# Tying the loads of h, and their squares, to the newest products in the MLP of a hybrid decoder layer

## The chip, the cores and the metric

The kernel runs on one core of a Trainium2 chip. The metric is the device time of one execution in microseconds (us); a lower time is better. Engines are named as in the profile: PE multiplies matrices, DVE is the vector engine, ACT the scalar engine (activations and copies out of PE's accumulators), POOL the general engine, SP issues most of the transfers.

## The reference, cut to what matters

One decoder layer over 2064 tokens (16 meta tokens and 2048 others) of width 1024, in 32-bit floats. A mixing half comes first (a gated convolution group beside a state-space group, a norm per group, one output projection, added to the residual stream). What follows is the half that the change touches:

```python
h = h + mixed @ w_out[i]                     # end of the mixing half
hn = rms_norm(h, norm_ffn_g[i])              # the norm ahead of the MLP
up = causal_dwconv(hn @ w_up[i], ffn_conv_w[i], ffn_conv_b[i])   # 2 x 2816 columns, width 3
a, val = up[..., :D_FF], up[..., D_FF:]
h = h + (silu(a) * val) @ w_down[i]
y = rms_norm(h, norm_final_g)                # the last norm
return y[:, N_META:]
```

`rms_norm` divides each token by the root of the mean of its 1024 squares and multiplies by a gain per column.

## The kernel before, in words

**Data.** Everything stands with features on the 128 partitions and tokens along the free dimension. The residual stream h lies in device memory as `h_d`, 128 partitions x 8 groups of features x 2064 tokens. The mixing half ends by storing h there (L957). The MLP adds its result to `h_d` by transfers that accumulate (L1510).

**Products.** Each 32-bit operand is split into a high part and a low remainder, and a product is three matmuls (high x high, high x low, low x high). Weights are loaded raw (`wr`), split by ACT into `wh` (L248) and by DVE into `wl` (L109), and then used. `Feed` keeps up to four split tiles and up to three raw ones ready (L1226 to L1266).

**The MLP** runs over three blocks of 676 or 688 tokens, each in two halves (columns c = 0 and 1). In a block, 22 feature tiles f are made by `up(f)`: seven forms of twelve matmuls each (a Strassen-like scheme with seven products instead of eight; X, Y, z1, z2 are accumulators), copied out by ACT (L1447, L1449, L1454, L1456) or added by DVE into the tiles `g` and `v` of the tag z. X and Y are used by several forms, so PE has to wait for their evictions. Then `activate` does the convolution, silu and the gate, and splits the outcome. Chunks of 4, 4, 4, 3, 3 and 4 tiles f are multiplied by w_down one chunk late: after the first `up` of chunk ci, `down(ci - 1, ...)` makes the eight output groups m (0 and 1 together, then one by one). ACT copies each to `ev` (L1506), and POOL issues the accumulating transfer to `h_d` (L1510).

**The norms beside it.** Small generators do the rest in the gaps; `prep` holds them in a queue, and `prep.step()` lets the first go on to its next `yield`. A step is made after each `up(f)` with f below 18 and after each down, two after the pair.
- `prep_rs(b)` (L1108) makes the inverse root mean squares of block b ahead of its MLP, one half after the other, through `inv_rms_from` (L216): two loads of h (L221), four yields, two squares in place by ACT (L227), three adds by DVE (L109), a sum over partitions by PE (`st_f`, L188), a power on POOL, and a broadcast by PE (`sb_f`, L208) that ACT copies to `rsk`. Block 0's runs in the mixing half, block 1's is queued before the MLP begins, block 2's in block 1.
- `finish(b)` (L1349) is the last norm of block b, run in the next block, again half by half: two loads (L1354), four yields, two squares into other buffers `ysq` (L1358), adds, `st_y`, `sb_y`, the scaling (L1369) and two stores to `y` (L1372). Block 2 has another way (L1375).
- `prep_mlp(b)` (L1122) loads h once more (L1134), scales it (L1139) and makes the split operands of the next block.

The loads' tiles and the squares share the tag "sq", a ring of four buffers in the MLP.

**What sets the order.** The program is traced in the order in which it is written, but each engine gets a list that a planner lays out when the program is built: it goes through the instructions with modelled durations, gives each engine what is ready in its model, prefers what stands earlier in the program, and fills an idle engine with what stands later. Dependences through data and buffers are kept by semaphores. At run time each list is worked through as it was laid out. So a load or a square may stand well ahead of its place in the program if nothing that it depends on forbids it.

Of the kernel before, what the change touches and what calls it, by code (L numbers as in the profile page):

```python
# [14 lines left out]
AF = mybir.ActivationFunctionType  # L15
ALU = mybir.AluOpType

P = 128
D = 1024
# [38 lines left out]
def layer_kernel(ctx, tc, xq, pk, w_in, w_glu, w_out, w_up, w_down, ssm_s, ssm_m, y):  # L58
    nc = tc.nc
    V, S, T, G = nc.vector, nc.scalar, nc.tensor, nc.gpsimd  # L60
    dma = nc.sync.dma_start
# [13 lines left out]
    h_d = dram.tile([P, KD, L], F32, name="h_d")  # L75
# [32 lines left out]
    def tt(out, a, b, op):  # L108
        V.tensor_tensor(out, a, b, op=op)  # L109
# [37 lines left out]
    def half_tile(n, name, tag="xt", bufs=3):  # L147
        return xp_.tile([P, 4, QM], F32, tag=tag, bufs=bufs, name=name)[:, :, :n]
# [32 lines left out]
    def inv_rms_of(s, nfeat, n, name, out=None, keep=False):  # L181
        sl, starts = slices(n)
        nj = len(starts)
        ps = aux_tile(f"st_{name}")
        terms = s if isinstance(s, list) else [s]
        for j, o in enumerate(starts):
            for i, a in enumerate(terms):
                T.matmul(  # L188
                    ps[:sl, j : j + 1], a[:, o : o + sl], ones[:, 0:1], start=i == 0, stop=i == len(terms) - 1
                )  # L190
        return (yield from inv_rms_at(ps[:sl, :nj], starts, nfeat, n, name, out, keep))
# [24 lines left out]
    def inv_rms_from(srcs, n, name, out=None):  # L216

        ts = []
        for i, src in enumerate(srcs):
            ts.append(half_tile(n, f"sq_{name}_{i}", tag="sq", bufs=SQ))  # L220
            dma(out=ts[i], in_=src)  # L221
        yield
        yield
        yield
        yield
        for t in ts:
            S.activation(t, t, AF.Square)  # L227
        a, b = ts
        tt(a, a, b, ALU.add)
        tt(a[:, 0:2, :], a[:, 0:2, :], a[:, 2:4, :], ALU.add)  # L230
        tt(a[:, 0, :], a[:, 0, :], a[:, 1, :], ALU.add)
        yield
        yield
        return (yield from inv_rms_of(a[:, 0, :], D, n, name, out))
# [58 lines left out]
    prep, ssm = Side(), Side()  # L293
# [812 lines left out]
    rs_f = [{} for _ in range(3)]  # L1106

    def prep_rs(b):  # L1108

        first, ni, _ = BLOCKS[b]  # L1110
        n = ni // 2
        rsk = rs_tile(f"rsk_{b}")
        for c in range(2):
            out = rsk[:, c, :n]
            s0 = first + c * n
            rs_f[b][c] = yield from inv_rms_from([h_d[:, i * 4 : i * 4 + 4, s0 : s0 + n] for i in range(2)], n, f"f{b}{c}", out)
            yield

    hf = [{} for _ in range(3)]
# [91 lines left out]
    for i in range(3):  # L1211
        c = C_FW + i * 44 + FT
# [131 lines left out]
    def y_at(b, c):  # L1344
        tb, ni, no = BLOCKS[b]
        n = no // 2
        return tb + ni - no + c * n, n

    def finish(b):  # L1349
        for c in range(2):  # L1350
            s0, n = y_at(b, c)
            xs, sq = ([half_tile(n, f"{k}_{b}_{c}_{i}", tag="sq", bufs=4) for i in range(2)] for k in ("y", "ysq"))
            for i, a in enumerate(xs):
                dma(out=a, in_=h_d[:, i * 4 : i * 4 + 4, s0 : s0 + n])  # L1354
            for _ in range(4):
                yield
            for a, q in zip(xs, sq):
                S.activation(q, a, AF.Square)  # L1358
            yield
            q = sq[0]  # L1360
            tt(q, q, sq[1], ALU.add)
            tt(q[:, 0:2, :], q[:, 0:2, :], q[:, 2:4, :], ALU.add)
            tt(q[:, 0, :], q[:, 0, :], q[:, 1, :], ALU.add)
            yield
            rs = yield from inv_rms_of(q[:, 0, :], D, n, f"y{b}{c}")
            yield
            for i, a in enumerate(xs):
                for k in range(4):
                    V.scalar_tensor_tensor(  # L1369
                        out=a[:, k], in0=a[:, k], scalar=col(C_FIN + 4 * i + k), in1=rs, op0=ALU.mult, op1=ALU.mult  # L1370
                    )
                dma(out=y[:, i * 4 : i * 4 + 4, s0 - META : s0 - META + n], in_=a)  # L1372
                yield
# [16 lines left out]
    def ev2_tile(name):  # L1390
        return fp.tile([P, MAX_OUT], F32, tag="ev2", bufs=3, name=name)

    prep.add(prep_rs(1))
    feed.pump()
    acc = []
    for b in range(3):
        tb, ni, no = BLOCKS[b]
        n, nn = ni // 2, no // 2
        o = 2 if b else 0
# [39 lines left out]
        def up(f, end=False):  # L1439
            g, v = (z_tile(f"z_{b}_{f}_{i}")[:, :nz] for i in range(2))  # L1440
            g2, v2 = two(g[:, o:]), two(v[:, o:])
            xy = xy_tile(f"xy_{b}_{f}")
            X, Y = xy[:, 0, :n], xy[:, 1, :n]
            z1, z2 = (ps_z.tile([P, 512], F32, tag="z", name=f"pz_{b}_{f}_{i}")[:, :n] for i in range(2))
            w = feed.take()
            form(X, w, 1, "b11", stop=False)
            S.activation(g2[:, 0, :], X, AF.Copy)  # L1447
            form(z2, w, 0, "t4")
            S.activation(v2[:, 0, :], z2, AF.Copy)  # L1449
            feed.done()  # L1450
            work()
            w = feed.take()
            form(Y, w, 0, "t1", stop=False)
            S.activation(v2[:, 1, :], Y, AF.Copy)  # L1454
            form(X, w, 1, "t2", start=False, stop=False)
            S.activation(g2[:, 1, :], X, AF.Copy)  # L1456
            feed.done()
            work()
            w = feed.take()
            form(Y, w, 0, "b22", start=False)  # L1460
            tt(g2[:, 1, :], Y, g2[:, 1, :], ALU.add)
            feed.done()
            w = feed.take()
            form(z1, w, 1, "b21")
            tt(g2[:, 0, :], z1, g2[:, 0, :], ALU.add)
            work()
            later.append(activate(f, (g, v)))
            form(X, w, 0, "t3", start=False)
            if end:
                work()  # L1470
            tt(v2, X.unsqueeze(1).to_broadcast([P, 2, n]), v2, ALU.add)
            feed.done()
            if f < f0_last:
                prep.step()

# [4 lines left out]
        def down(ci, ms, cs=(0, 1), into=None):  # L1480

            f0, nk = chunk_of[ci]
            todo, whole = [], {}
            for i, m in enumerate(ms):
                name = f"dn_{b}_{ci}_{m}_{cs[0]}"
                if i < 2:
                    ps = xy_tile(name)
                    whole[m] = ps[:, :, :nn]
                    ps = [ps[:, c, :nn] for c in cs]
                else:  # L1490
                    ps = [ps_z.tile([P, 512], F32, tag="z", name=f"{name}_{c}")[:, :nn] for c in cs]
                todo.append((m, ps, feed.take()))

            def rhs_down(k, i):
                return tuple(a[:, cs[i] * nn : (cs[i] + 1) * nn] for a in act[f0 + k])

            for ks in (range(nk - 1), range(nk - 1, nk)) if len(ms) > 1 else (range(nk),):
                for m, ps, w in todo:
                    product(ps, w, rhs_down, nk, ks=ks)
            for m, ps, _ in todo:  # L1500
                feed.done()
                s0 = tb + ni - no
                if into is None:
                    ev = ev2_tile(f"ev_{b}_{ci}_{m}")[:, :no]
                    if m in whole:
                        S.activation(two(ev), whole[m], AF.Copy)  # L1506
                    else:
                        for c in cs:
                            S.activation(two(ev)[:, c], ps[c], AF.Copy)
                    G.dma_start(out=h_d[:, m, s0 : s0 + no], in_=ev, accum_op=ALU.add)  # L1510
                else:
                    for i, c in enumerate(cs):
                        tt(into(m, c), ps[i], into(m, c), ALU.add)

        first_pair = [(0, 1)] + [(m,) for m in range(2, KD)]
        for ci, (f0, nk) in enumerate(chunk_of):
            if ci == last and b < 2:
                prep.drain()
                prep.add(prep_mlp(b + 1, hf[b + 1]))
            for f in range(f0, f0 + nk):  # L1520
                up(f, f == f0 + nk - 1 and ci == last)
                if f == f0 and ci:
                    for ms in first_pair:
                        down(ci - 1, ms)
                        work()
                        prep.step(len(ms))
            if ci == last:
                settle()
# [11 lines left out]
        else:  # L1540
            s0, _ = y_at(b, 0)
            for i in range(4):
                t = f32(hl_tile(QM, f"acc_{i}", **(xh2 if i < 2 else {})))
                for m in range(2):
                    dma(
                        out=t[:, 2 * m : 2 * m + 2, :nn],
                        in_=h_d[:, 2 * i + m, s0 : s0 + no].rearrange("p (c t) -> p c t", c=2),
# [6 lines left out]
            for c in range(2):  # L1554
                s = half_tile(nn, f"tail_sum{c}", tag="sq", bufs=4)[:, 0, :]
                for ms in first_pair if c == 0 else [(m,) for m in range(KD)]:
                    down(last, ms, (c,), rows)
                    for m in ms:
                        q = s if m == 0 else z_tile(f"tq_{c}_{m}")[:, :nn]
# [90 lines left out]
```

## Time and profile before

| | |
|---|---|
| median of 3 runs | 2223.89 us (2220.8 to 2225.02) |
| the profiled execution | 2220.69 us, its span 2218.9 us |
| PE busy | 2121.5 us, 96% of the span |
| DVE, ACT busy | 1682.3 us (76%), 1102.1 us (50%) |
| mean granted clock of PE | 0.98 |
| MLP | from about 745 us to the end |

The rows of the profile give times from the start of the span. A row of waits reads: engine, output and line that waited, what ended the wait, total us, number, longest. A group of instructions reads: line, engine, operation, output <- inputs, shapes, count, then busy us and mean ns of one, then idle time of the engine before them. Tiles carry the program's names: `y`, `ysq` and `sq_f` are the tiles of the norms, `z` and `ev` those of up and down. L109 and L248 are helpers that many places call, so tiles tell more than lines there. A transfer's row on SP is its issue; it lands later.

### The profile page before, as it was taken

What the parts mean: (1) busy time and instruction counts of PE and PEld (TensorE: products, weight loads), DVE (VectorE), ACT (ScalarE), POOL (GpSimd) and SP (SyncE); (2) the same over time, 40 slices, a digit from 0 to 9 for tenths busy, and PEclk for the clock granted to TensorE, in tenths of its full rate; (3) what the DMA queues carried; (4) which work ended last, traced back from release to release, by engine and by line L of the source; (5) the groups of instructions that cost most, each with busy time, mean ns of one, the idle gap of its engine ahead of it and who ended that gap; (6) DMA issues with size and microseconds to landing.
All of it is one profiled execution on the core that took longest, in us unless ns stands there. A gap on an engine that the chain in (4) does not pass through costs nothing. (4 is left out here: it accounts for less than half of the span.)

```text
span 2218.9 us, 33122 instructions
## 1 busy us (share of the span) xinstructions
PE 2121.5 (96%) x13012; PEld 2061.5 (93%) x13012; DVE 1682.3 (76%) x2507; ACT 1102.1 (50%) x1651; POOL 151.4 (7%) x174
## 2 busy tenths in 40 slices
PE   7997999999899999999999899899999899999996
PEld 7997999998899999999999899899999899999996
DVE  8896499858956887686768869677868868667776
ACT  4135333337423555465556555455556555455555
POOL 0000000000000000100111010100111010110000
PEclk9998999999999999999999999999999999999998
DMA  7376544351576334624555262733555262653463
GB/s 241 108 219 164 145 149 150 108 178 53 162 233 202 134 105 120 142 80 112 129 130 130 91 169 76 211 107 87 139 128 141 82 170 62 158 120 95 101 170 113
DMA packets 170749, 300.28 MB, mean 135 GB/s; under 512 B 32416, under 2 KB 104800, under 8 KB 170464
## 3 DMA queue, kind: packets, MB, share of 16 engines
q1 hardware_dynamic: 149856, 246.41, 35.9%
q0 software_dynamic: 19584, 47.52, 12.6%
q10 hardware_dynamic: 1152, 4.23, 0.5%
q8 instruction: 102, 1.67, 0.3%
q14 instruction: 55, 0.45, 0.1%
HBM read 214.29 MB, written 83.82 MB: 134 GB/s over the span
## 5 line engine op out<-in xcount | busy, mean ns | idle before, releaser
L109 DVE TENSOR_TENSOR wl_up<-wr_up,wh_up 128x1024 fp32r<-128x1024 f32 x198 | 241.6, 1222 | 138.7 <-ACT wh_up L248 132.8
L138 PE MATMUL dn<-ah,wh_dn 128*128 128x344 f32 (+1 forms) x1024 | 327.8, 324 | 10.4 <-ACT ah L248 8.9
L139 PE MATMUL dn<-al,wh_dn 128*128 128x344 f32 (+1 forms) x1024 | 324.7, 320 | 0.4 <-DVE al L109 0.3
L248 ACT ACTIVATE wh_up<-wr_up 128x1024 fp32r<-128x1024 f32 x198 | 209.5, 1059 | 197.3 <-DVE wr_up L109 53.1
L1409 PE MATMUL xy<-h_t,wh_up 128*128 128x344 f32 (+1 forms) x792 | 263.9, 333 | 12.9 <-ACT z L1447 7.9
L1411 PE MATMUL xy<-h_t,wl_up 128*128 128x344 f32 (+1 forms) x792 | 254.0, 321 | 0.0
L1410 PE MATMUL xy<-l_t,wh_up 128*128 128x344 f32 (+1 forms) x792 | 253.7, 320 | 0.0
L142 PE MATMUL dn<-ah,wl_dn 128*128 128x344 f32 (+1 forms) x1024 | 247.3, 320 | 0.0
L138 PEld LDWEIGHTS dn<-ah,wh_dn 128*128 128x128 f32 x1024 | 193.6, 190 | 14.4 <-ACT ah L248 9.7
L1510 POOL DMA_DIRECT2D h_d<-ev x136 | 118.3, 870 | 1233.5 <-ACT ev L1506 1221.0
L139 PEld LDWEIGHTS dn<-al,wh_dn 128*128 128x128 f32 x1024 | 194.2, 190 | 1.8 <-DVE al L109 1.0
L1409 PE MATMUL xy<-h_b,wh_up 128*128 128x344 f32 (+1 forms) x528 | 176.5, 335 | 13.7 <-ACT z L1456 12.2
L1409 PEld LDWEIGHTS xy<-h_t,wh_up 128*128 128x128 f32 x792 | 149.8, 189 | 30.7 <-ACT z L1454 16.4
L142 PEld LDWEIGHTS dn<-ah,wl_dn 128*128 128x128 f32 x1024 | 178.1, 190 | 0.0
L1410 PE MATMUL xy<-l_b,wh_up 128*128 128x344 f32 (+1 forms) x528 | 169.9, 322 | 0.0
L1411 PE MATMUL xy<-h_b,wl_up 128*128 128x344 f32 (+1 forms) x528 | 168.6, 322 | 0.0
L248 ACT ACTIVATE wh_dn<-wr_dn 128x512 fp32r<-128x512 f32 (+1 forms) x144 | 85.5, 594 | 134.7 <-issue 52.5
L1410 PEld LDWEIGHTS xy<-l_t,wh_up 128*128 128x128 f32 x792 | 150.6, 190 | 0.0
L1411 PEld LDWEIGHTS xy<-h_t,wl_up 128*128 128x128 f32 x792 | 150.4, 190 | 0.0
L115 DVE SCALAR_TENSOR_TENSOR g<-z,pv,g 128x688 f32<-128x688 f32 (+1 forms) x132 | 122.3, 927 | 22.9 <-ACT g L1414 22.2
L109 DVE TENSOR_TENSOR wl_dn<-wr_dn,wh_dn 128x512 fp32r<-128x512 f32 (+1 forms) x144 | 92.5, 644 | 58.7 <-ACT wh_dn L248 57.4
L115 DVE SCALAR_TENSOR_TENSOR v<-z,pneg,v 128x688 f32<-128x688 f32 (+1 forms) x132 | 122.4, 928 | 9.4 <-ACT v L1414 8.1
(401 smaller groups left out, 5361.9 us busy)
## 6 DMA issues: line engine op xcount, KB each, us to landing
wr_up<-in_w_up SPq DMA_DIRECT2D x132, 512.0 KB, 5.4
h_d<-ev POOLq DMA_DIRECT2D x88, 344.0 KB, 6.8
wr_dn<-in_w_down SPq DMA_DIRECT2D x96, 256.0 KB, 2.7
wr_cw<-in_w_in SPq DMA_DIRECT2D x36, 512.0 KB, 4.5
h_d<-ev POOLq DMA_DIRECT2D x48, 336.0 KB, 6.6
x_c<-in_xq SPq DMA_DIRECT2D x16, 688.0 KB, 6.4
wr_dn<-in_w_down SPq DMA_DIRECT2D x48, 192.0 KB, 2.3
xr<-in_xq SPq DMA_DIRECT2D x24, 344.0 KB, 3.9
```

The costliest lines, as they stand in the source:

```text
L109: V.tensor_tensor(out, a, b, op=op)
L115: V.scalar_tensor_tensor(out=out, in0=a, scalar=s, in1=b, op0=ALU.mult, op1=ALU.add)
L138: T.matmul(ps[c], hi[:, k, :], xh, start=k == 0, stop=False)
L139: T.matmul(ps[c], hi[:, k, :], xl, start=False, stop=False)
L142: T.matmul(ps[c], lo[:, k, :], xh, start=False, stop=k == nk - 1)
L248: S.activation(hi, t, AF.Copy)
L1409: T.matmul(ps, hi[:, j, :], xh[:, j, :], start=start and j == 0, stop=False, **kw)
L1410: T.matmul(ps, hi[:, j, :], xl[:, j, :], start=False, stop=False, **kw)
L1411: T.matmul(ps, lo[:, j, :], xh[:, j, :], start=False, stop=j == 3, **kw)
L1510: G.dma_start(out=h_d[:, m, s0 : s0 + no], in_=ev, accum_op=ALU.add)
```

## The change

`hold(t)` copies one column of `mark[0]`, a product, into the first column of a tile that is then overwritten: the load or the square that fills the tile has to come after the copy, and the copy after the product. `mark[0]` is set anew, as the program is traced, by each `up` (a column of its tile `g`, which DVE writes at L1465 of before) and by each `down` that stores (a column of `ev`). `norm_h` is the part of `finish` from its loads to its inverse root mean squares, with a hold ahead of each load and of each square. `finish` calls it, and `prep_rs` calls it for blocks 1 and 2, which so square into buffers of their own and not in place. `prep_rs(1)` is queued after `up(0)` of block 0 and no longer ahead of the MLP; its first step then follows `up(1)`.

```diff
@@ prep_rs @@
-            rs_f[b][c] = yield from inv_rms_from([h_d[:, i * 4 : i * 4 + 4, s0 : s0 + n] for i in range(2)], n, f"f{b}{c}", out)
+            srcs = [h_d[:, i * 4 : i * 4 + 4, s0 : s0 + n] for i in range(2)]
+            if b == 0:
+                rs_f[b][c] = yield from inv_rms_from(srcs, n, f"f{b}{c}", out)
+            else:
+                _, rs_f[b][c] = yield from norm_h(srcs, n, f"f{b}{c}", out)
             yield
@@ ahead of finish @@
+    mark = [None]
+
+    def hold(t):
+
+        V.tensor_copy(t[:, 0, 0:1], mark[0])
+
+    def norm_h(srcs, n, name, out=None):
+
+        xs, sq = ([half_tile(n, f"{k}_{name}_{i}", tag="sq", bufs=4) for i in range(2)] for k in ("y", "ysq"))
+        for a, src in zip(xs, srcs):
+            hold(a)
+            dma(out=a, in_=src)
+        for _ in range(4):
+            yield
+        for a, q in zip(xs, sq):
+            hold(q)
+            S.activation(q, a, AF.Square)
+        yield
+        q = sq[0]
+        tt(q, q, sq[1], ALU.add)
+        tt(q[:, 0:2, :], q[:, 0:2, :], q[:, 2:4, :], ALU.add)
+        tt(q[:, 0, :], q[:, 0, :], q[:, 1, :], ALU.add)
+        yield
+        rs = yield from inv_rms_of(q[:, 0, :], D, n, name, out)
+        return xs, rs
@@ finish @@
-            ...
-            rs = yield from inv_rms_of(q[:, 0, :], D, n, f"y{b}{c}")
+            srcs = [h_d[:, i * 4 : i * 4 + 4, s0 : s0 + n] for i in range(2)]
+            xs, rs = yield from norm_h(srcs, n, f"y{b}{c}")
@@ ahead of the loop over blocks @@
-    prep.add(prep_rs(1))
     feed.pump()
@@ up, at its end @@
             tt(v2, X.unsqueeze(1).to_broadcast([P, 2, n]), v2, ALU.add)
             feed.done()
+            mark[0] = g[:, o : o + 1]
             if f < f0_last:
                 prep.step()
@@ down, where it stores @@
                     G.dma_start(out=h_d[:, m, s0 : s0 + no], in_=ev, accum_op=ALU.add)
+                    mark[0] = ev[:, 0:1]
@@ loop over f @@
                 up(f, f == f0 + nk - 1 and ci == last)
+                if b == f == 0:
+                    prep.add(prep_rs(1))
```

More of the change, by code (lines that the diff above doesn't have):

```diff
@@ L1351, in finish @@
             s0, n = y_at(b, c)
[L1352 to L1364, printed above, removed]
-            rs = yield from inv_rms_of(q[:, 0, :], D, n, f"y{b}{c}")
+            srcs = [h_d[:, i * 4 : i * 4 + 4, s0 : s0 + n] for i in range(2)]
+            xs, rs = yield from norm_h(srcs, n, f"y{b}{c}")
             yield
```

## The prediction

> **What bounds the kernel now.** I read the page's busy shares, then the busy time by windows, then the waits inside the windows where TensorE falls short, then the timeline of the worst of these.
>
> ```profile
> span 2218.9 us, 33122 instructions
> PE 2121.5 (96%) x13012; PEld 2061.5 (93%) x13012; DVE 1682.3 (76%) x2507; ACT 1102.1 (50%) x1651; POOL 151.4 (7%) x174
> ```
>
> PE sets the end; the other engines matter only where they make it wait. The columns below are the stretch, its length, each engine's busy time with its count of instructions, the granted clock, the DMA share and GB/s.
>
> ```profile
> 735.00:795.00 60.00, 56.48 (x351) 54.34 (x351) 50.34 (x63) 39.65 (x55) 0.00 (x0) 1.00 0.40 134
> ...
> 1215.00:1245.00 30.00, 24.37 (x144) 23.79 (x143) 17.48 (x21) 14.54 (x25) 0.86 (x1) 0.89 0.55 156
> 1318.00:1340.00 22.00, 19.14 (x120) 18.47 (x119) 13.40 (x19) 12.26 (x19) 1.72 (x2) 1.00 0.71 185
> 1408.00:1435.00 27.00, 19.89 (x114) 19.20 (x113) 14.07 (x18) 10.08 (x18) 2.33 (x3) 0.87 0.77 221
> 1712.00:1742.00 30.00, 24.27 (x141) 23.80 (x140) 16.91 (x20) 14.54 (x23) 0.86 (x1) 0.89 0.52 147
> 1818.00:1838.00 20.00, 17.61 (x100) 16.85 (x99) 10.59 (x14) 9.57 (x14) 1.13 (x2) 0.91 0.62 159
> 1435.00:1555.00 120.00, 120.00 (x747) 116.86 (x746) 91.78 (x122) 67.22 (x121) 8.69 (x10) 1.00 0.39 97
> 1840.00:2000.00 160.00, 159.89 (x997) 156.26 (x996) 116.55 (x153) 85.49 (x138) 14.74 (x17) 1.00 0.48 116
> ```
>
> The last two are quiet stretches of the MLP: 747 matmuls in 120 us and 997 in 160 us, both 6.23 per us. The five middle ones fall short of that rate. In each, PE waits once for an eviction by ACT, and ACT has been waiting for a load of h or for a buffer of the norm:
>
> ```profile
> PE xy L1409 <- ACT z L1456: 5.6, 1, 5.6
> ...
> ACT ysq L1358 <- DMA y<-h_d: 7.4, 1, 7.4
> ...
> PE xy L1409 <- ACT z L1454: 2.9, 1, 2.9
> ...
> ACT ysq L1358 <- issue: 3.1, 1, 3.1
> ACT ysq L1358 <- DMA out_y<-y: 2.4, 1, 2.4
> ...
> PE xy L1409 <- ACT z L1447: 7.1, 1, 7.1
> ...
> ACT sq_f L227 <- DMA sq_f<-h_d: 7.8, 1, 7.8
> ...
> PE xy L1409 <- ACT z L1456: 5.7, 1, 5.7
> ...
> ACT ysq L1358 <- DMA y<-h_d: 7.6, 1, 7.6
> ...
> PE xy L1409 <- ACT z L1454: 2.1, 1, 2.1
> ...
> ACT ysq L1358 <- DMA out_y<-y: 5.3, 2, 3.6
> ```
>
> These are the five windows in order. The timeline of the third shows how one such wait works (start, duration, engine, line, operation; the bracket is the idle time before it):
>
> ```profile
> 1411.49 0.38 SPq L221 DMA_DIRECT2D sq_f<-h_d  x1
> ...
> 1413.48 0.32 PE L1411 MATMUL xy<-h_b,wl_up 128*128 128x344 f32 x1
> ...
> 1415.38 0.32 PE L1411 MATMUL pz<-h_t,wl_up 128*128 128x344 f32 x1
> 1421.06 1.35 ACT L227 ACTIVATE sq_f<-sq_f 128x1376 f32<-128x1376 f32 x1 [7.75 <-DMA sq_f<-h_d]
> 1422.31 0.44 ACT L1447 ACTIVATE z<-xy 128x344 f32<-128x344 f32 x1
> ...
> 1422.81 0.65 PE L1409 MATMUL xy<-h_t,wh_up 128*128 128x344 f32 x1 [7.11 <-ACT z L1447]
> ...
> 1423.26 0.49 PE L1410 MATMUL xy<-l_t,wh_up 128*128 128x344 f32 x1
> ```
>
> The product that L1447 evicts was finished before 1414, but L1447 stands behind the square in ACT's list, and the square's load was issued only at 1411.49 and landed 9.5 us later. PE ran dry at 1415.7. When it resumed, a matmul row lasted 0.49 us instead of 0.32: the window's clock is 0.87, so some time is lost after the idle gap too. That is why I price a stall by the matmuls missing from its window, not by its gap.
>
> **The change part by part.**
>
> *Loads and squares are held* (L1116, L1354, L1358 of before). Every pair of loads and every pair of squares in the norms named by the diff, except block 0's own norm, gets a copy of one column first. It reads what the newest products left: a column of z, which DVE itself wrote, or of ev, which ACT evicted. The plan can no longer put the load or the square ahead of that point. The program has four steps between a load and its square, and from the code these are:
> - last norm of a block, first half: load after up(0), square after up(4), four ups;
> - its second half: load after the last down of chunk 0, square after up(8), four ups;
> - norm ahead of block 2: load after up(9), square after the first pair of downs of chunk 2, three ups and a pair; its second half, one down and three ups.
>
> An up is 7 forms of 12 matmuls, 84/6.23 = 13.5 us; a down of four tiles is 24 matmuls, 3.9 us. The shortest distance is therefore 3.9 + 3 x 13.5 = 44 us, against these landings of the loads (min/median/max, first L1354, then L221):
>
> ```profile
> DMA to landing us min/median/max: 4.0/4.5/6.9
> ...
> DMA to landing us min/median/max: 4.0/5.3/9.5
> ```
>
> So no square should meet its load any more. The waits for out_y go too: the second half's load now comes one down after the first half's last store was issued, and its squares reuse those buffers four ups later. The gain is what the five windows lack at 6.23 matmuls per us:
> - 30 us ask for 186.9, 144 are there: 42.9/6.23 = 6.9 us
> - 22 us ask for 137.1, 120: 2.7 us
> - 27 us ask for 168.2, 114: 8.7 us
> - 30 us ask for 186.9, 141: 7.4 us
> - 20 us ask for 124.6, 100: 3.9 us
>
> The sum is 29.6 us. The five gaps alone are 5.6 + 2.9 + 7.1 + 5.7 + 2.1 = 23.4 us; the remaining 6.2 are mostly half-speed matmuls behind them. [...] I keep 29.6.
>
> *The copies.* Eight per norm of two halves, four norms (ahead of blocks 1 and 2, last of blocks 0 and 1): 32. The nearest row is a copy of two columns; the row below it gives how long DVE has to wait for a product of PE, the next two how long ACT and DVE wait for each other:
>
> ```profile
> L913 DVE COPY halo<-cvt 128x2 f32<-128x2 f32 x12 | 2.0, 165 | 0.0
> ...
> DVE z L109 <- PE xy L1411: 40.5, 45, 1.8
> ...
> ACT wh_up L248 <- DVE wr_up L109: 53.1, 41, 2.7
> ...
> DVE wl_up L109 <- ACT wh_up L248: 137.8, 80, 5.0
> ```
>
> 32 x 0.165 = 5.3 us of DVE, in a stage where DVE idles 28.2 of 120 us (the quiet window): I take 0. Ten of the sixteen pairs read z, which DVE finished earlier in its own list, so they wait for nothing new. Six read ev: loads after m = 6 or 7, squares after m = 1. Such a copy can hold DVE until ACT has evicted that product. Behind it stand the splits of weights (L109, wl), for which PE waits; PE has up to four split tiles in hand, at 3.9 us a tile in a down. I take 0. If that cover is gone, six waits of one down, 6 x 3.9 = 23 us, are the bound. On SP the held loads stand ahead of weight loads, but those wait for the same DVE list.
>
> *Squares as a pair.* Before, the landings kept a pair apart; now both become ready at once:
>
> ```profile
> L227 ACT ACTIVATE sq_f<-sq_f 128x1376 f32<-128x1376 f32 x8 | 10.8, 1350 | 13.4 <-DMA sq_f<-h_d 13.4
> L1358 ACT ACTIVATE ysq<-y 128x1376 f32<-128x1376 f32 x4 | 5.4, 1352 | 12.9 <-DMA y<-h_d 7.6 <-DMA out_y<-y 5.3
> ```
>
> Two are 2.7 us on ACT. A form is 12/6.23 = 1.9 us, and the tightest eviction (L1454, between t1 and b22) has one form to spare. Eight pairs cost between 0 and 8 x 1.35 = 10.8 us, one square late each; as the plan still puts evictions first when both are ready, I take 0.3 us each, 2.4.
>
> *The norm ahead of block 1 starts after up(0)*, not at the phase's start. Four squares and some adds leave the window 735 to 795, which lacks 22.8 matmuls, 3.7 us. I found no PE wait for them there, so I take 0 (bounds: 0 to a gain of 3.7).
>
> *Other buffers.* This norm now takes four buffers of the ring of four instead of two, so the loads of the next block's h (L1134) can't be pulled as far ahead; they come when its second half's sums are through (in block 1, in the downs after up(15)). They are needed for the block's last downs, six ups or 81 us later. Cost 0; that distance is the cover, and gone it would cost one landing of at most 9.5 us a block.
>
> Sum: -29.6 + 2.4 = -27.2 us. The profiled execution took 2220.69 us, 1.8 over its span; that gives 2193.5. The median of the runs is 2223.89, 3.2 higher, and the forecast is for such a median: 2223.9 - 27.2 = 2197 us. Its own range is 2190 (ramp gained, squares free) to 2205 (squares at 10.8).
>
> **The rivals.**
>
> *A: the wait changes hands.* ACT no longer waits for the load but for the copy, which stands behind splits in DVE's list. The longest wait of ACT on DVE in the row above is 2.7 us; with 2.7 us of squares, less the 1.9 us of one form, 3.5 us per pair. If half of the eight pairs are hit, 14 us return: about 2211 us. For it: DVE is 76% busy and these waits are frequent. Against: they hardly reach PE in the quiet windows.
>
> *B: slower, DVE held by the copies.* Each of the sixteen pairs stops DVE until a product is through, and weights run out at PE. It decides from 29.6/16 = 1.85 us of lost PE time per pair; if each costs as much as the 2.9 us gap did (2.7 us), the time is 2223.9 - 29.6 + 43.7 = 2238. [...] Against: ten pairs read DVE's own result, DVE's longest wait for xy in the row above is 1.8 us, and PE has tiles in hand.
>
> *C: nothing comes of it.* The planner lays out all lists anew, and other loads or evictions take the five places; or a held load still meets its square, because the plan pulls other work past it. Time 2220 to 2228. Against: the five gaps are the largest in the MLP up to the tail, all have this one form, and the data order forbids it.
>
> **How the numbers follow.** Forecast 0.70, A 0.14, C 0.08, B 0.08. Runs of this kernel tell about 0.2% (4.4 us) from no change. The forecast and A lie beyond that on the fast side: faster 0.84; C is the same: 0.08; B: slower 0.08. For 8 in 10 the range takes all of the forecast's own range and most of A: 2189 to 2213.
>
> **What would show it.** In the windows around the starts of the ups that follow a block's start and a down phase, PE's waits for L1447, L1454 and L1456 should fall below 1 us, and the granted clock should stay at 1.00 there. ACT's waits for y<-h_d, out_y and, inside the MLP, for the squared loads should vanish. Squares should start at least 40 us after their loads. Copies should last 0.16 us with short idle times before them; long ones, released by ACT ev, are B; ACT squares released by the copy are A. I am wrong if the MLP still holds stalls of 20 us together, or if PE starves for weights behind a copy.

## The result, and the profile after

The changed kernel takes 2198.06 us (median of 4 runs) against 2223.28 us before (4 runs): ratio 0.989, 95% interval 0.9874 to 0.9906, a gain of 25.2 us. The forecast was 2197 us. The profiled execution took 2199.40 us, with a span of 2197.6 us. Two executions of later runs lie far outside all others (2419.42 us of the kernel before, 7209.57 us of the changed kernel) and are left out of the medians and ratios below.

The busy times of the changed kernel:

```profile
span 2197.6 us, 33162 instructions
...
PE 2119.1 (96%) x13012; PEld 2057.7 (94%) x13012; DVE 1688.0 (77%) x2539; ACT 1097.5 (50%) x1651; POOL 153.2 (7%) x174
```

PE does the same 13012 matmuls in nearly the same busy time; the span is shorter mainly by what PE no longer waits. DVE has 32 instructions more, the copies. The windows below are those of the prediction, moved to where the same matmuls now run, in the prediction's order: the ramp, the five short windows, then one new short window, then the quiet stretch (columns as before: length, busy time and count of each engine, clock, DMA share, GB/s).

```profile
735.00:795.00 60.00, 56.96 (x347) 55.25 (x346) 48.08 (x62) 33.55 (x48) 0.00 (x0) 0.97 0.29 97
1218.50:1248.50 30.00, 30.00 (x186) 28.93 (x185) 22.81 (x31) 16.25 (x30) 0.86 (x1) 1.00 0.52 145
1315.00:1337.00 22.00, 22.00 (x138) 21.36 (x137) 14.51 (x21) 11.38 (x19) 1.73 (x2) 1.00 0.82 235
1401.50:1428.50 27.00, 27.00 (x168) 25.96 (x166) 19.39 (x28) 14.72 (x27) 1.73 (x2) 1.00 0.73 208
1703.50:1733.50 30.00, 30.00 (x186) 28.97 (x185) 23.16 (x31) 16.31 (x27) 0.86 (x1) 1.00 0.52 140
1802.00:1822.00 20.00, 20.00 (x126) 19.38 (x125) 12.49 (x18) 10.46 (x17) 1.29 (x2) 1.00 0.80 235
1548.00:1573.00 25.00, 20.40 (x116) 19.48 (x116) 16.70 (x26) 9.71 (x16) 3.46 (x4) 0.93 0.75 182
...
1840.00:2000.00 160.00, 159.91 (x997) 156.05 (x996) 116.97 (x157) 85.55 (x136) 14.79 (x17) 1.00 0.49 117
```

All five windows are full: PE is busy for their whole length at clock 1.00. They hold 186 - 144, 138 - 120, 168 - 114, 186 - 141 and 126 - 100 matmuls more, 185 in all, and 185/6.23 = 29.7 us. The seventh row is a stall that the kernel before did not have. Its window asks for 25 x 6.23 = 155.8 matmuls and holds 116, 6.4 us short; before, the same place was almost full:

```profile
1562.00:1587.00 25.00, 24.68 (x151) 23.57 (x150) 20.00 (x30) 12.29 (x20) 3.77 (x5) 1.00 0.82 197
```

That is 0.8 us short, so 5.6 us are new. 29.7 - 5.6 = 24.1 us; the profiled executions differ by 2220.69 - 2199.40 = 21.3 us and the medians by 25.2. The 2.8 us between fit what was lost ahead of the first window, which begins 3.5 us later than before, and most of that loss changes from run to run: the first matmul behind PE's wait of 2.9 us at the end of block 0 starts at 1192.66 us before and at 1196.53 here, but at 1192.44 in the profile of the run with every copy twice (below) and at 1194.73 in a second profile of the changed kernel. The changed kernel's groups of copies and of squares, and the landings of the held loads (L1365):

```profile
L1358 DVE COPY ysq_y<-z 128x1 f32<-128x1 f32 x8 | 0.8, 145 | 0.0
...
L1358 DVE COPY ysq_f<-ev 128x1 f32<-128x1 f32 x4 | 0.4, 150 | 0.0
...
L1358 DVE COPY y_y<-ev 128x1 f32<-128x1 f32 x4 | 0.4, 145 | 0.0
...
L1370 ACT ACTIVATE ysq_f<-y_f 128x1376 f32<-128x1376 f32 x8 | 10.5, 1348 | 0.9 <-DVE ysq_f L1358 0.9
...
L1370 ACT ACTIVATE ysq_y<-y_y 128x1376 f32<-128x1376 f32 x4 | 5.4, 1348 | 2.0 <-DVE ysq_y L1358 2.0
...
DMA to landing us min/median/max: 4.7/8.1/11.1
```

A copy lasts 0.15 us and DVE has no idle time before it where it reads `ev` (of the four groups that read `z` none has more than 0.1 us in all). No held square waits for a load or for a store of y any more; in five of the eight pairs ACT waits about 1 us for the copy, and PE has no wait for an eviction into `z` left in the MLP.

**The new stall.** What PE and DVE waited for in the new window, then DVE's and ACT's timelines there:

```profile
PE xy L1427 <- ACT ev L1525: 4.6, 1, 4.6
...
DVE v_b L1143 <- DMA v_b<-h_d: 6.3, 1, 6.3
...
1547.28 1.06 DVE L1143 SCALAR_TENSOR_TENSOR v_b<-v_b,pv,rsk 128x344 f32<-128x344 f32 x2
1554.64 1.55 DVE L1143 SCALAR_TENSOR_TENSOR v_b<-v_b,pv,rsk 128x344 f32<-128x344 f32 x3 [6.30 <-DMA v_b<-h_d]
...
1552.39 0.74 ACT L1525 ACTIVATE ev<-dn 128x688 f32<-128x688 f32 x1 [0.28 <-DMA h_d<-ev]
1560.64 1.06 ACT L248 ACTIVATE wh_up<-wr_up 128x1024 fp32r<-128x1024 f32 x1 [7.50 <-DVE wr_up L109]
1561.60 0.73 ACT L1525 ACTIVATE ev<-dn 128x688 f32<-128x688 f32 x1
```

DVE stands for 6.3 us in front of the scaling of the next block's h (L1143), whose load has not landed. Behind it are the sums of weights (L109, `wr_up`), for which ACT's split waits 7.5 us, and behind that split in ACT's list is the eviction of `ev` that PE needs. It is the old pattern on another engine: a later stage's work, planned right behind its load, stops the list of an engine that PE lives on. In block 0 DVE stands at the same line for 4.6 us, but amid downs, and PE is busy all through (window 912 to 924):

```profile
920.82 2.04 DVE L1143 SCALAR_TENSOR_TENSOR v_b<-v_b,pv,rsk 128x344 f32<-128x344 f32 x4 [4.63 <-DMA v_b<-h_d]
...
912.00:924.00 12.00, 12.00 (x78) 11.80 (x77) 6.32 (x14) 3.72 (x7) 3.43 (x4) 1.00 1.04 266
```

### The profile page after: what moved, and what is told of

Its sections match the earlier page's. It is cut to its first block, busy times and chain, and to the rows that moved or that the text cites. A ratio compares the mean times of both kernels' runs of the same rounds, so it can differ in the third digit from the quotient of the medians.

```text
span 2197.6 us, 33162 instructions
## 1 busy us (share of the span) xinstructions
PE 2119.1 (96%) x13012; PEld 2057.7 (94%) x13012; DVE 1688.0 (77%) x2539; ACT 1097.5 (50%) x1651; POOL 153.2 (7%) x174
## 4 chain that ended last, share of the span: by engine, by line
PE 60%; issue 8%; DVE 5%; ACT 3%; DMA 3%; POOL 1%; SPq 0%; POOLq 0%; DVEq 0%; ACTq 0%
PE xy L1427 9%; PE xy L1429 8%; PE xy L1428 8%; PE dn L138 6%; PE dn L139 6%; PE dn L142 6%; PE pz L1429 3%; PE pz L1427 3%; PE pz L1428 3%; PE po L138 2%; PE po L142 2%; PE po L139 1%; DMA v_b<-h_d 1%; DMA gt<-g_d 1%; ACT h_ms L1038 1%
## 5 line engine op out<-in xcount | busy, mean ns | idle before, releaser
L109 DVE TENSOR_TENSOR wl_up<-wr_up,wh_up 128x1024 fp32r<-128x1024 f32 x198 | 241.8, 1222 | 140.7 <-ACT wh_up L248 138.5
L109 DVE TENSOR_TENSOR wl_dn<-wr_dn,wh_dn 128x512 fp32r<-128x512 f32 (+1 forms) x144 | 92.3, 644 | 45.6 <-ACT wh_dn L248 44.9
```

## The experiments

All but the last, which repeats it, are edits of the changed kernel, and all are timed against the kernel before on the same chip.

**Copies ahead of the squares alone.**

```diff
         for a, src in zip(xs, srcs):
-            hold(a)
             dma(out=a, in_=src)
```

> The changed kernel with the copies ahead of the squares alone; the loads of h are free again. Theory (ACT stood at squares whose data was not there; holding the square is what counts): no square waits for a load of h, the five windows stay filled, about 2198 us (2193 to 2203). Rival (the gain came from loads that no longer stand early in SP's list ahead of weight loads): about half of the 25 us comes back, 2205 to 2215, with waits of PE for weights.

Measured: 2198.83 us, ratio 0.9895 (0.9879 to 0.9912). ACT's waits at the squares of the MLP are the same as in the changed kernel, and none is for a load:

```profile
ACT ysq_y L1369 <- DVE ysq_y L1358: 4.1, 4, 1.0
...
ACT ysq_f L1369 <- DVE ysq_f L1358: 0.9, 1, 0.9
```

The loads stand early again (the first of the last norm leaves at 1209.8 us, against 1230.9 in the changed kernel and 1211.8 before), and nothing is lost. Holding the squares is enough; the rival, in which the loads were in the way of weights, falls.

**Copies ahead of the loads alone.**

```diff
         for a, q in zip(xs, sq):
-            hold(q)
             S.activation(q, a, AF.Square)
```

> The changed kernel with the copies ahead of the loads alone; the squares may be planned as early as the modelled landing allows. Theory: ACT stands at squares again, one landing (4 to 10 us) less what the plan allows for it, at up to eight pairs; PE loses 10 to 25 us of the 30 gained, 2208 to 2223 us. Rival (the late place of the loads is the gain): 2198 us.

Measured: 2215.5 us, ratio 0.9969 (0.9958 to 0.9979); two thirds of the gain are gone. ACT's waits in the MLP, then the four waits of PE behind the worst of them:

```profile
ACT ysq_f L1369 <- DMA y_f<-h_d: 12.9, 5, 4.7
...
ACT ysq_y L1369 <- DMA y_y<-h_d: 9.6, 2, 5.0
...
PE xy L1426 <- ACT z L1464: 3.8, 1, 3.8
...
PE xy L1426 <- ACT z L1473: 3.4, 1, 3.4
...
PE xy L1426 <- ACT z L1464: 4.1, 1, 4.1
...
PE xy L1426 <- ACT z L1473: 2.9, 1, 2.9
```

The squares stand behind their loads again, now at later places, and seven of them stop ACT for 22.5 us together. Holding a load alone moves the stall with it. The two runs together show which half of the copies works.

**Copies in the last norm alone**, the norm ahead of the MLP as before (squares in place, two buffers a half).

```diff
-            if b == 0:
-                rs_f[b][c] = yield from inv_rms_from(srcs, n, f"f{b}{c}", out)
-            else:
-                _, rs_f[b][c] = yield from norm_h(srcs, n, f"f{b}{c}", out)
+            rs_f[b][c] = yield from inv_rms_from(srcs, n, f"f{b}{c}", out)
```

> The changed kernel with the old norm ahead of the MLP (no copies there, squares in place, two buffers a half); the last norm keeps its copies. Theory (each held square removes its own stall; the stall before L1427 that is new in the changed kernel, 6 us, comes from the norm ahead of the MLP taking four buffers): the four stalls at ysq stay away, the one at sq_f (9 us of PE) is back somewhere, the new one is gone: 2223 - 21 = 2202 us (2197 to 2207). Rival (the plan is laid out anew and stalls fall where they will): a new stall of DVE at v_b stays, about 2208 us or more.

Measured: 2201.81 us, ratio 0.9904 (0.989 to 0.9919). The third stall is back, as large as it was, and the new window is nearly full:

```profile
PE xy L1424 <- ACT z L1462: 7.0, 1, 7.0
...
ACT sq_f L227 <- DMA sq_f<-h_d: 7.6, 1, 7.6
...
1548.00:1573.00 25.00, 23.82 (x146) 22.85 (x146) 17.37 (x29) 11.60 (x20) 5.95 (x7) 1.00 0.97 218
```

That is 146 matmuls in place of 116. So holding the norm ahead of the MLP gains its own 9 us and costs most of the new stall's 6 us; the net of the two fits the 3 to 4 us that separate this run from the changed kernel.

**Copies in the norm ahead of the MLP alone**: `norm_h` without holds where `finish` calls it.

```diff
-            xs, rs = yield from norm_h(srcs, n, f"y{b}{c}")
+            xs, rs = yield from norm_h(srcs, n, f"y{b}{c}", held=False)
```

> The changed kernel without the copies in the last norm; the norm ahead of the MLP keeps its copies and its four buffers. Theory: the four stalls at ysq are back (21 us of PE in the trace of before), the one at the norm ahead of the MLP stays away (9 us) and the stall at v_b stays (6 us): 2223 - 9 + 6 = 2220 us (2214 to 2224). Rival (one stall removed frees the lists for the others too): below 2212 us.

Measured: 2219.33 us, ratio 0.9993 (0.9982 to 1.0005), not to be told from before. The windows of the four stalls of the last norm are short again, and the one of the norm ahead of the MLP is full:

```profile
1218.00:1248.00 30.00, 24.68 (x145) 23.87 (x144) 20.29 (x26) 14.70 (x25) 0.00 (x0) 0.94 0.40 111
1318.00:1340.00 22.00, 18.73 (x109) 18.45 (x108) 12.19 (x17) 10.42 (x17) 1.73 (x2) 0.92 0.64 155
1712.00:1742.00 30.00, 24.44 (x139) 23.76 (x139) 18.24 (x21) 14.07 (x24) 0.86 (x1) 0.89 0.49 141
1818.00:1838.00 20.00, 16.90 (x103) 15.86 (x103) 11.39 (x15) 10.34 (x15) 0.86 (x1) 1.00 0.55 143
1398.00:1425.00 27.00, 27.00 (x168) 26.36 (x168) 16.65 (x27) 11.23 (x18) 4.35 (x5) 1.00 0.83 197
```

The new stall is in this run too, which takes most of the 9 us that the full window is worth:

```profile
PE xy L1429 <- ACT ev L1527: 4.6, 1, 4.6
...
DVE v_b L1143 <- DMA v_b<-h_d: 6.5, 1, 6.5
```

So the stalls of each norm go with the copies of that norm, most of the new stall comes with the norm ahead of the MLP, and the gains add up within the spread of the runs: against before, the two halves of the change bring 21.2 and 2.7 us, the whole 25.2.

**Every copy twice.**

```diff
         V.tensor_copy(t[:, 0, 0:1], mark[0])
+        V.tensor_copy(t[:, 0, 1:2], mark[0])
```

> The changed kernel with every copy made twice: 64 in place of 32. Theory (the copies cost nothing on the path): 2198 us (2194 to 2202). Rival (the copies hold DVE, and part of the gap between the 30 us gained and the 25 us measured is their price): 5 us more, 2203 us or above.

Measured: 2198.2 us, ratio 0.9896 (0.9878 to 0.9914). 32 more copies cost nothing that can be measured, so they are not where the new 6 us come from.

**The scaling of the next block's h held too**, through a small tile of its gains.

```diff
+        gains = [pv[:, C_FFN : C_FFN + KD]]
...
-                    out=a, in0=a, scalar=col(C_FFN + 4 * i + j), in1=rs_f[b][c], op0=ALU.mult, op1=ALU.mult
+                    out=a, in0=a, scalar=gains[0][:, 4 * i + j : 4 * i + j + 1], in1=rs_f[b][c], op0=ALU.mult, op1=ALU.mult
...
         yield
         yield
+        if b:
+            gains[0] = xp_.tile([P, KD], F32, tag="gf", bufs=1, name=f"gf_{b}")
+            V.tensor_copy(gains[0][:, 0:1], mark[0])
+            V.tensor_copy(gains[0], pv[:, C_FFN : C_FFN + KD])
```

> The changed kernel, and beside it the scaling of the next block's h (L1143) takes its gains from a small tile that is filled behind a copy of the newest product, so the scaling can't be planned ahead of the downs of chunk 4. Theory (the new stall is DVE standing at v_b, planned right behind its load): the 6 us stall goes, about 2192 us (2188 to 2196). Rival (the burst of loads itself starves the split of weights there): the stall stays, 2196 to 2201 us; or DVE is late at the end of the block, where the scaling now stands, above 2201.

Measured: 2196.44 us, ratio 0.9884 (0.9869 to 0.9899), at the border of the two expectations; the time alone does not set this run apart from the changed kernel. In the trace DVE no longer stands at `v_b`, but part of the stall stays:

```profile
PE xy L1433 <- ACT ev L1531: 2.7, 1, 2.7
...
DVE wr_up L109 <- DMA wr_up<-in_w_up: 3.8, 1, 3.8
...
1548.00:1573.00 25.00, 22.31 (x137) 21.37 (x136) 13.18 (x17) 10.84 (x18) 4.33 (x5) 1.00 0.81 200
```

What DVE waits for now is raw weights, 3.8 us: four loads of h, 688 KB each, are issued in the 10 us (1533.3 to 1543.4) in which the turn from downs to ups wants its weights.

**The loads of the next block's h held as well, one per step in the downs of chunk 4**, on top of the last edit.

```diff
+            if b:
+                hold(v[k])
             dma(out=v[k], in_=h_d[:, i * 4 : i * 4 + 4, s0 : s0 + n])
...
-        load("b12", 0, 1)
-        load("b22", 1, 1)
-        load("b21", 1, 0)
-        yield
-        yield
+        for k, i, c in (("b12", 0, 1), ("b22", 1, 1), ("b21", 1, 0)):
+            if b:
+                yield
+            load(k, i, c)
+        yield
+        yield
```

> As the run with held gains, and the four loads of the next block's h are held as well, one per step in the downs of chunk 4, so they no longer come in a burst when the ring's buffers come free. Theory (in the run with held gains 2.7 us of the stall stayed because four loads of 704 KB in a row made the weights late): the window after the downs of chunk 3 in block 1 loses nothing; against the changed kernel 6 us less, 2190 to 2194 us. Rival (the burst only moves, or the scaling is now late for the block's end): 2196 us or more, with a stall in the downs of chunk 4 or at the end of block 1.

Measured: 2209.6 us, ratio 0.995 (0.9934 to 0.9966): the rival. The stall left its place and came back larger after the downs of chunk 4, in both blocks (PE's and DVE's waits in block 1, then in block 0):

```profile
PE xy L1436 <- ACT ev L1534: 5.4, 1, 5.4
...
DVE wr_up L109 <- DMA wr_up<-in_w_up: 7.5, 1, 7.5
...
PE xy L1436 <- ACT ev L1534: 7.4, 1, 7.4
...
DVE wr_up L109 <- DMA wr_up<-in_w_up: 9.2, 1, 9.2
```

The theory named the cause, late weights, rightly, but its remedy was wrong: one load per down is still four loads at a turn from downs to ups.

**The same loads held to two ups in the middle of the block**, two behind each; the scaling stands in the downs that follow.

```diff
+        if b:
+            while not in_up[0]:
+                yield
         load("b11", 0, 0)
         load("b12", 0, 1)
+        if b:
+            yield
+            while not in_up[0]:
+                yield
         load("b22", 1, 1)
         load("b21", 1, 0)
...
-                prep.drain()
-                prep.add(prep_mlp(b + 1, hf[b + 1]))
+                while 1 not in rs_f[b + 1]:
+                    prep.step()
```

`prep_mlp` is queued behind `prep_rs`, and `in_up` is true during the step that follows an up.

> As the run with held gains, but the four loads of the next block's h are held to two ups in the middle of the block (two loads behind each of two ups, not in the downs), and the scaling stands in the downs that follow. Theory (an h load that meets the turn from downs to ups makes the raw weights late there, 2.7 us in the run with held gains and 5.5 to 7.4 us in the run that held these loads in the downs): no gap of PE over 2 us is left between the two gaps at L138 that end the blocks, other than those; 6 us under the changed kernel, 2190 to 2194 us. Rival (the weights were late for another reason): a gap of 2 us or more stays after the downs of chunk 3 in block 1, 2195 us or more.

Measured: 2193.64 us, ratio 0.9868 (0.9847 to 0.9888). The new window is full, and PE has no wait in it:

```profile
1548.00:1573.00 25.00, 25.00 (x155) 24.18 (x154) 15.58 (x21) 12.72 (x21) 3.79 (x5) 1.00 0.83 190
```

Beside the same runs of before, the changed kernel as it is:

> The changed kernel once more, as it is, on the same chip and beside the same runs of before, so that the version with loads in the ups can be set against it: 2194 to 2201 us, with the gap of 4.6 us after the downs of chunk 3 in block 1 again.

Measured: 2198.6 us (median of 5 runs), ratio 0.9891 (0.9868 to 0.9914), with its 4.6 us gap of PE again. The version with the loads in the ups is 5.0 us faster by the medians; the two intervals overlap, so the times alone do not prove it, but the stall that it was made for is gone from the trace.

## Why the prediction was right, and where it was not

**The gain.** Forecast 29.6 us from matmuls missing in five windows, measured 29.7 us in the same windows. Pricing by missing matmuls and not by gaps (23.4 us) was the right choice: the time at half speed behind the gaps (before, the granted clock is 0.50 from 1422.8 to 1426.0 us, behind the gap of 7.1 us) came back too.

**Loads and squares.** The prediction held that no square meets its load; it was right, with squares 41 us or more behind the issue of their loads. It did not say which copies do the work. The squares' copies do it alone; the loads' copies alone bring 7.5 us.

**Copies.** Taken at 0 and bounded at 23 us by DVE standing before `ev`. Next to no idle time stands before them (at most 0.1 us a group), and doubling them changed nothing (2198.2 us against 2198.06). Rival B, DVE held by the copies, did not happen. Rival A happened in the small: ACT waits for a copy, 5.0 us in five of eight pairs, but none of it reaches PE.

**Squares as a pair.** Taken at 2.4 us, bounds 0 to 10.8. The window 1840 to 2000 now holds a pair, at 1856, and the same 997 matmuls as before without one, so that pair cost about 0; the other seven were not priced one by one, but no wait of PE for an eviction into `z` is left.

**The ramp.** Taken at 0. The window 735 to 795 holds 347 matmuls where it held 351, at clock 0.97 in place of 1.00, so nothing was won there.

**Other buffers.** This is the step that failed. It read "Cost 0; that distance is the cover", six ups between the late loads of the next block's h and their use, and put one landing of at most 9.5 us a block behind it if the cover was gone. The distance stood in the program, but the plan does not use it: it pulls the scaling right behind its load, as it had pulled the squares. The ring's buffers came free late: the first two loads of the burst leave at 1531.82 and 1533.48 us, right behind the squares that read their buffers (1530.43 and 1532.11). The longest landing of these loads rose from 6.9 to 13.2 us (landings of `v_b`, before, then after), and DVE stood 6.3 us:

```profile
DMA to landing us min/median/max: 4.1/5.1/6.9
...
DMA to landing us min/median/max: 4.1/6.1/13.2
```

The price was 5.6 us in block 1, within the bound that the step had named and set aside. The runs show two parts of it: DVE at the scaling (gone when the gains are held, 137 matmuls in place of 116 in the window, 3.4 us) and weights late behind the burst (137 to 155, 2.9 us, gone when the loads stand in the ups).

That the sum came out about 1 us from the median is in part luck: two terms missed in opposite directions, 2.4 us for the squares that were not paid and 5.6 us for the buffers that were. With both put right the sum is 2223.9 - 29.7 + 5.6 = 2199.8 us, also inside the spread of the runs. Against its own forecast for the profiled execution, 2193.5 us, the prediction was 5.9 us too low: 3.2 us by these two terms, the rest fits what was lost ahead of the first window.

**The sign of being wrong.** By the letter one of the prediction's signs appeared, stalls of 20 us together in the MLP: PE's waits from 745 us to the end add up to 23.2 us. It was set without counting the waits at the start of the MLP, at the ends of the blocks and in the tail, which made up 17.8 of the 42.8 us before. The waits for evictions into `z`, which the change was made for, fell from 25.0 us to nothing.

## What to carry to other kernels

Where a planner fills idle time with work whose data it believes to be there, tie the consumer that blocks an engine to a product of the main chain: here ACT stood 7.8 us at a square whose load had not landed, with an eviction behind it in its list, and DVE 6.3 us at a scaling. Check the same for every later stage whose buffers the change delays: six ups of distance in the program did not keep the plan from pulling that scaling forward. Such a tie of one column cost nothing that could be measured here, even where it read what another engine had to evict first. Mind where the transfers of a side job stand: with the four loads of the next block's h at a turn from downs to ups, DVE waited 3.8 us for raw weights though nothing waited for those loads, and 7.5 and 9.2 us with one load per down; behind two ups in the middle of the block they left the window full, 155 matmuls in 25 us.

## What the runs showed of the hardware that was not expected

Behind some gaps PE ran at half speed for a few us: in the kernel before the granted clock is 0.50 from 1422.8 to 1426.0 us, and the matmuls start 0.29 us apart there in place of 0.16. That did not follow from the gap's length alone. At the end of block 0 the profiles before and after have the same wait of PE, and the window's clock is 0.94 in both. Here it is, with its window, in the run with copies ahead of the loads alone, in which the clock stays full there, then in the run with held gains:

```profile
PE dn L138 <- ACT ah L248: 2.9, 1, 2.9
...
1185.00:1215.00 30.00, 27.00 (x174) 26.45 (x173) 26.95 (x27) 19.30 (x26) 4.40 (x6) 1.00 0.50 127
...
1185.00:1215.00 30.00, 27.00 (x165) 26.45 (x163) 27.56 (x29) 19.54 (x27) 4.33 (x5) 0.94 0.51 130
```

The same gap of 2.9 us leaves the window's clock at 1.00 in the one and at 0.94, with nine matmuls fewer (1.4 us), in the other. The ramp's window shows the same with a longest wait of 1.6 us (before, then after), at clock 1.00 before and 0.97 after in the rows shown (0.50 from 756.8 to 760.0 us after):

```profile
PE pz L1409 <- ACT wh_up L248: 1.6, 1, 1.6
...
PE pz L1427 <- ACT wh_up L248: 1.6, 1, 1.6
```

The gap of 2.1 us in the prediction's fifth window also had half-speed matmuls behind it (clock 0.91 in the window, 0.52 from 1828.8 to 1832.3 us), and the one of 2.9 us in its second window had none (1.00). No run here shows what decides it.

One consequence for timing: a stall of 2.1 to 2.9 us cost its gap plus nothing to 1.8 us here (nothing in the second window, 1.4 us above, 3.9 - 2.1 in the fifth), and the same wait of 2.9 us came both ways.
